# Splitting q after its trip through DRAM, GpSimd's block sums written earlier, and the last norm with squares summed by TensorE

## The chip, the core and the metric

The kernel runs on one core of a Trainium2 chip. The metric is the time of one execution in device microseconds. TensorE (PE in the profile) multiplies, with a separate lane for weight loads (PEld); VectorE (DVE), ScalarE (ACT) and GpSimd (POOL) work on tiles of 128 partitions; SyncE (SP) only issues DMAs here. Each engine runs its own instructions in order and waits for the others through semaphores.

## The reference

One layer of a streaming encoder on 1024 tokens of 1024 channels, float32. `proj` is one wide projection of the normed input; branch A is a gated short convolution, branch B a convolution of width 31 with a layer norm; both are gated, merged and projected, and an FFN and a last norm follow.

```python
h = rms_norm(x, norm_mix_g[l]) * (1.0 + sc1) + sh1
proj = jnp.einsum('bsd,de->bse', h, w_in[l])
b_s, c_s, v_s, v_c, gl_c, gate_br = jnp.split(proj, SPLITS[:-1], axis=-1)

y_a = b_s * causal_dwconv(c_s * v_s, conv_short_w[l])
y_a = jnp.einsum('bsc,cd->bsd', y_a, w_short_out[l])

u = v_c * jax.nn.sigmoid(gl_c)
u = causal_dwconv(u, conv_conf_w[l]) + conv_conf_b[l]
u = jax.nn.silu(layer_norm(u, conf_ln_g[l], conf_ln_b[l]))
y_b = jnp.einsum('bsc,cd->bsd', u, w_conf_out[l])
g_a, g_b = jnp.split(jax.nn.sigmoid(gate_br), 2, axis=-1)
mix = jnp.einsum('bsd,de->bse', g_a * y_a + g_b * y_b, w_o[l])
x = x + g1 * mix

h2 = rms_norm(x, norm_ffn_g[l]) * (1.0 + sc2) + sh2
a, bgate = jnp.split(jnp.einsum('bsd,df->bsf', h2, w_ffn_in[l]), 2, axis=-1)
x = x + g2 * jnp.einsum('bsf,fd->bsd', jax.nn.silu(a) * bgate, w_ffn_out[l])
return rms_norm(x, final_norm_g)
```

`rms_norm(x, g)` is `x * rsqrt(mean(x * x) + EPS) * g`. What the text calls q is `b_s * causal_dwconv(c_s * v_s, conv_short_w)`, the input of `w_short_out`.

## The kernel before

**Three products for one.** Every float32 operand of a matmul is split into a hi part (rounded to the type that TensorE multiplies in one pass, `F32R`) and a lo part (what is left); a block is then hi x hi, lo x hi and hi x lo (`mm3`, lines 281 to 292; the matmuls are those of lines 289, 290 and 292). Weights are split by `split_w` (lines 202 to 212): ScalarE casts a tile of 128 x 1024 to `wh` (line 208), and another engine subtracts it to give `wl` (line 209). `wh` and `wl` have three buffers each, and `next_w` keeps two units ahead of the one in use, so the split of a unit begins when the product three places before it has let go of its buffer.

**The duals.** Most of the input projection is done in twelve duals (lines 722 to 728), each a pair of column blocks multiplied with seven block products in place of eight, in the order `PRODUCTS = "1265734"`. `dual_units` (lines 214 to 238) makes the weights of each product: "1" and "2" are blocks 11 and 12 themselves; "6", "5" and "7" need sums of blocks (`s1` = 21 + 22, 21 + 11, 11 + `s1`, lines 231 to 233), "3" needs 12 + 11 (line 235). All four blocks are loaded when unit "1" is fetched. In the duals of the input projection the lo parts and the sums run on GpSimd (`eng=nc.gpsimd`, line 244), in the FFN's on VectorE. The results leave PSUM through `win_evac` (lines 567 to 631), on ScalarE and VectorE.

**Beside the duals.** VectorE also computes the long convolution (`conv`, lines 648 to 677), whose taps are strung out behind the reads of PSUM, one instruction a tap (line 663); each convolution ends with two ScalarE instructions (line 676), and GpSimd adds it to a running total (`add_conv`, line 683, tile `tot`).

**q.** Four of the pairs are of kind "q". When such a pair's last product is read, the tiles `sc[j]` and `sc[j + 1]` hold q, and `q_store` (lines 541 to 548) splits each half on the spot: ScalarE casts it into a new tile `qs` (line 545), GpSimd subtracts (line 546), and SyncE stores hi and lo together (line 548), 16 stores of 512 KB. In the last dual `q_load` (lines 635 to 638) brings back hi and lo as two loads of 256 KB each, 32 in all, four (j, h) pairs after each of the first four products; the tiles they go to are those that the duals' operands leave. They are the operands of the first product after the duals, `ya` (line 758).

**The end.** The last part of the FFN's output is computed in three pieces of 512, 256 and 256 tokens (`PIECES`), eight steps of 128 channels each (`piece_out`, lines 1069 to 1086): twelve matmuls, an evacuation on VectorE (line 1078), a square on ScalarE (line 1081), and, for what GpSimd will scale, the gain on ScalarE (line 1085). VectorE sums the eight squares (`piece_sum`, line 1090), TensorE sums them over channels with a matrix of ones (`norm_start`, line 410, tile `ss`), ScalarE takes the reciprocal root (line 339), and VectorE refines it in three instructions (`rstd_end`, lines 344 to 346). `piece_scale` (lines 1092 to 1106) multiplies, on GpSimd for the first two pieces and for steps 0, 3 and 5 of the last one (line 1101), else on VectorE (line 1103), and stores in pairs. The norm of a piece is started inside the next piece, after step `NORM_AT` = 2, and finished after step 5; the last piece's comes behind everything.

**What sets the order.** A planner lays out each engine's instructions from the order in which they are written and from when it expects their inputs; `tc.issue_after` puts an instruction behind a given one on the same engine. What is written later can be placed earlier if it is ready earlier.

Of the kernel before, what the change touches and what calls it, by code (L numbers as in the profile page):

```python
# [39 lines left out]
P = 128  # L40
D = 1024
T = 1024
H = 512
# [44 lines left out]

NORM_AT = 2
LAG = 2
POOL_LAST = (0, 3, 5)


# [8 lines left out]
PIECES = [(0, 512), (512, 256), (768, 256)]  # L104


FILL = 272


@with_exitstack  # L110
def block_kernel(ctx: ExitStack, tc: tile.TileContext, x0, xT, c, vecs, ada, w_first, w_plain, w_duals,
# [75 lines left out]
    def raw_tile(n=1024):  # L187

        raws.append(raws.pop(0))
        return raws[-1].tile([P, 1024], F32, tag="raw", name="raw")[:, :n]  # L190
# [23 lines left out]
    def dual_units(mats, n, early=False, eng=nc.vector):  # L214

        a = {}

        def get(*blocks):
            for b in blocks:
                a[b] = load(mats[("11", "12", "21", "22").index(b)], n)  # L220

        def unit(m):
            if early:
                get(*{"1": ("11",), "2": ("12",), "6": ("21", "22", "11"), "3": ("12",), "4": ("22",)}.get(m, ()))
            elif m == "1":
                get("11", "12", "21", "22")
            if m in "12":
                return split_w(a["1" + m], n, (), eng)
            if m == "6":
                a["s1"] = a["22"] if early else raw_tile(n)  # L230
                eng.tensor_tensor(a["s1"], a["21"], a["22"], ALU.add)  # L231
                eng.tensor_tensor(a["21"], a["21"], a["11"], ALU.add)
                eng.tensor_tensor(a["11"], a["11"], a["s1"], ALU.add)
            elif m == "3":
                eng.tensor_tensor(a["12"], a["12"], a["11"], ALU.add)
            return split_w(a[{"6": "11", "5": "s1", "7": "21", "3": "12", "4": "22"}[m]], n, (), eng)

        return {m: (lambda m=m: unit(m)) for m in PRODUCTS}
# [178 lines left out]
    def uc_tile(name, n=T + CK - 1, dt=F32):  # L417
        return ucp.tile([P, T + CK - 1], dt, tag="uc", name=name)[:, :n]
# [120 lines left out]
    q_dram = {}  # L539

    def q_store(j):

        for h in range(2):
            s = uc_tile("qs", T, F32R)
            nc.scalar.copy(s[:, :H], sc[j][:, halves[h]])
            nc.gpsimd.tensor_tensor(s[:, H:], sc[j][:, halves[h]], f32(s[:, :H]), ALU.subtract)
            q_dram[j, h] = dram.tile([P, T], F32, name=f"q{j}{h}")
            nc.sync.dma_start(q_dram[j, h], f32(s))

    def short_conv(j, p):  # L550
        sc[j] = uc_tile(f"sc{j}", T)
# [82 lines left out]

    def q_load(j, h):
        qT[j][h] = t_pair(f"q{j}{h}")
        for t, s in zip(qT[j][h], halves):
            nc.sync.dma_start(f32(t), q_dram[j, h][:, s])


    taps = vec[:, V_CW : V_CW + CK // 2 * 2 * KC].rearrange("p (j two k) -> p j two k", two=2, k=KC)
# [80 lines left out]
    for d in range(n_duals):  # L722
        banks, evac = {}, win_evac(PAIRS[2 * d : 2 * d + 2])
        for i, m in enumerate(PRODUCTS):
            product(banks, m, th[m], evac, y_tile=ps_tile)
            if d == n_duals - 1:
                for n in range(4 * i, min(4 * i + 4, 2 * KC)):
                    q_load(n // 2, n % 2)

    zs = {}  # L730

# [244 lines left out]
    def in_product(d, m):  # L976
        product(in_banks[d], m, ts[m], in_evac(d), y_tile=ps_tile if d == 1 else ps2_tile)
        if d == N_IN - 1:
            group_load(0, m)

    def norm_2_start():
        nonlocal r2
# [86 lines left out]
    def piece_out(i, j):  # L1069
# [12 lines left out]
        if i == LAST and j == KC - 1:  # L1082
            load_rsqrt(act.ins)
        if on_pool(i, j):
            nc.scalar.activation(dst, dst, AF.Copy, scale=col(V_GFIN, j))
        sqs.append(sq)

    def piece_sum(i, j):
# [3 lines left out]
    def piece_scale(i, rf):  # L1092
        at, n = PIECES[i]
        m = H // n
        for j in range(0, KC, m):
            ys = wide_tile("y") if m > 1 else x1[j][:, at : at + n]
            ys = ys.rearrange("p (m n) -> p m n", n=n)
            for d in range(m):
                y, src = ys[:, d], x1[j + d][:, at : at + n]
                if on_pool(i, j + d):  # L1100
                    nc.gpsimd.tensor_tensor(y, src, rf, ALU.mult)
                else:
                    nc.vector.scalar_tensor_tensor(
                        out=y, in0=src, scalar=col(V_GFIN, j + d), in1=rf, op0=ALU.mult, op1=ALU.mult
                    )
            nc.sync.dma_start(outT[j : j + m, :, at : at + n].rearrange("m p n -> p m n"), ys)

    def piece_norm(i, acc):
        return norm_start(acc, "rf", PIECES[i][1], wide_tile)

    for i in range(len(PIECES)):
        acc, sqs = sqs[0] if i else None, []
        lag = LAG if i == LAST else 0
        for j in range(KC):
            piece_out(i, j)
            if j > lag:
                piece_sum(i, j - lag)
            if i and j == NORM_AT:
                norm = piece_norm(i - 1, acc)
            if i and j == NORM_AT + 3:  # L1120
                with tc.issue_after(piece_out.ins):
                    rf = rstd_end(*norm)
                piece_scale(i - 1, rf)
        for j in range(KC - lag, KC):
            piece_sum(i, j)
    piece_scale(LAST, rstd_end(*piece_norm(LAST, sqs[0])))


def _chunks(v):
# [69 lines left out]
```

## Time and profile before

| | |
|---|---|
| median of 3 runs | 1516.14 us (1514.99 to 1517.78) |
| the profiled execution | 1518.37 us, of which the span is 1516.6 us |
| instructions in it | 17958 |
| mean granted TensorE clock | 0.992 |

The span goes from the first to the last instruction of the profiled execution. In rows of a timeline the first number is the start in us from the span's start, the second the duration, and in brackets stands the idle time of the engine before it and what ended it; in groups of the page stand count, busy us and mean ns of one. In rows of windows stand, behind the window and its length, the busy time and count of PE, PEld, DVE, ACT and POOL, then the granted clock, the DMA engines' busy share and GB/s.

The duals of the input projection run from about 128 to 585 us, the product `ya` follows, and the three pieces of the end take the last 50 us.

### The profile page before, as it was taken

The page shows a single profiled execution, that of the slowest core. Times are in us where ns is not written, and L with a number is a line of the kernel's source. Part 1 is how long each engine was busy: PE and PEld are TensorE (multiplying, and loading weights), DVE is VectorE, ACT ScalarE, POOL GpSimd, SP SyncE. Part 2 cuts the span into 40 slices and gives each one's busy share as a digit, 9 for nine tenths or more (in the row PEclk, how much of TensorE's full clock was granted, in tenths as well). Part 3 has the DMA queues.
Part 4 walks back from the last instruction along what each step waited for, and adds up shares of the span by engine and source line. Part 5 has one row for each costly group of instructions (what it writes and reads, how often), then busy time and mean ns, then how long its engine had stood idle before and what let it go on. Part 6 is the DMA issues. An engine that isn't in the chain of part 4 may idle for free.

```text
span 1516.6 us, 17958 instructions
## 1 busy us (share of the span) xinstructions
PE 1480.1 (98%) x6529; PEld 1211.6 (80%) x6529; DVE 1177.6 (78%) x1566; ACT 612.7 (40%) x871; POOL 582.0 (38%) x483
## 2 busy tenths in 40 slices
PE   9999999999998999999999989999999999999996
PEld 5788887877886888888788868888888888888886
DVE  7897898999998881858877798777777665676756
ACT  4654333433332442335335464444444443212234
POOL 0037788788768884320121001000111016535005
PEclk9999999999999999999999999999999999999998
DMA  9512223223222159647765436455554449999303
GB/s 345 207 63 84 84 70 139 70 97 111 98 83 87 66 198 393 242 152 223 251 207 163 143 97 193 156 179 179 181 172 158 155 152 365 354 292 282 124 15 112
DMA packets 87307, 255.66 MB, mean 169 GB/s; under 512 B 10033, under 2 KB 12209, under 8 KB 87218
## 3 DMA queue, kind: packets, MB, share of 16 engines
q1 hardware_dynamic: 46384, 146.30, 28.9%
q0 software_dynamic: 36944, 95.44, 19.1%
q10 hardware_dynamic: 3890, 12.78, 2.1%
q8 instruction: 51, 0.84, 0.2%
q14 instruction: 38, 0.31, 0.1%
HBM read 187.89 MB, written 66.58 MB: 168 GB/s over the span
## 4 chain that ended last, share of the span: by engine, by line
PE 50%; DVE 1%; ACT 1%; issue 0%; DVEq 0%; ACTq 0%
PE x L289 7%; PE x L290 7%; PE x L292 7%; PE z L289 4%; PE z L290 4%; PE z L292 4%; PE y L290 3%; PE y L289 3%; PE y L292 3%; PE mix L289 2%; PE mix L290 2%; PE mix L292 2%; PE yb L289 1%; PE yb L290 1%; PE yb L292 1%
## 5 line engine op out<-in xcount | busy, mean ns | idle before, releaser
L208 ACT CAST wh<-raw 128x1024 fp32r<-128x1024 f32 (+2 forms) x257 | 259.1, 1009 | 422.9 <-PE x L290 107.3
L209 POOL TENSOR_TENSOR wl<-raw,wh 128x1024 fp32r<-128x1024 f32 x92 | 238.0, 2594 | 86.5 <-ACT wh L208 80.1
L209 DVE TENSOR_TENSOR wl<-raw,wh 128x1024 fp32r<-128x1024 f32 (+2 forms) x165 | 188.2, 1141 | 52.4 <-ACT wh L208 50.2
L663 DVE SCALAR_TENSOR_TENSOR c<-diff,vec,c 128x512 f32<-128x512 f32 x248 | 182.3, 749 | 6.4 <-DMA q<-qs 2.6
L942 POOL DMA_DIRECT2D hid<-stage x71 | 37.9, 534 | 356.5 <-DVE stage L329 351.0
L289 PE MATMUL x<-th,wh 128*128 128x512 f32 x336 | 130.8, 389 | 0.0
L292 PE MATMUL x<-th,wl 128*128 128x512 f32 x336 | 130.7, 389 | 0.0
L290 PE MATMUL x<-tl,wh 128*128 128x512 f32 x336 | 130.7, 389 | 0.0
L663 DVE SCALAR_TENSOR_TENSOR c<-u,wsum,c 128x512 f32<-128x512 f32 x112 | 84.0, 750 | 7.1 <-issue 5.1
L292 PE MATMUL x<-t2h,wl 128*128 128x512 f32 x184 | 72.9, 396 | 4.2 <-POOL wl L209 4.2
L289 PE MATMUL x<-t2h,wh 128*128 128x512 f32 x184 | 72.2, 394 | 2.8 <-ACT t2h L328 2.4
L289 PEld LDWEIGHTS x<-th,wh 128*128 128x128 f32 x336 | 63.1, 188 | 13.3 <-issue 0.2
L290 PEld LDWEIGHTS x<-tl,wh 128*128 128x128 f32 x336 | 63.1, 188 | 13.1
L292 PEld LDWEIGHTS x<-th,wl 128*128 128x128 f32 x336 | 63.1, 188 | 13.1
L290 PE MATMUL x<-t2l,wh 128*128 128x512 f32 x184 | 72.5, 394 | 0.0
L231 POOL TENSOR_TENSOR raw<-raw 128x1024 f32<-128x1024 f32 x12 | 29.3, 2439 | 99.5 <-DVE wl L209 95.7
L292 PE MATMUL z<-th,wl 128*128 128x512 f32 x168 | 65.5, 390 | 0.0
L289 PE MATMUL z<-th,wh 128*128 128x512 f32 x168 | 65.4, 389 | 0.0
L290 PE MATMUL z<-tl,wh 128*128 128x512 f32 x168 | 65.4, 389 | 0.0
L328 ACT CAST stage<-g 128x512 fp32r<-128x512 f32 x62 | 38.3, 621 | 56.4 <-DMA hid<-stage 33.4
L270 DVE CUSTOM_DVE_ANT_0 raw<-raw,cs,vec 128x1024 f32<-128x1024 f32 x24 | 34.1, 1424 | 32.3 <-DMA raw<-in_ada 20.0
L329 DVE TENSOR_TENSOR stage<-g,stage 128x512 fp32r<-128x512 f32 x62 | 42.3, 687 | 21.7 <-ACT stage L328 21.6
(799 smaller groups left out, 4095.3 us busy)
## 6 DMA issues: line engine op xcount, KB each, us to landing
hid<-stage POOLq DMA_DIRECT2D x71, 512.0 KB, 4.8
raw<-in_w_fi SPq DMA_DIRECT2D x50, 512.0 KB, 4.2
raw<-in_w_duals SPq DMA_DIRECT2D x48, 512.0 KB, 3.5
th<-hid POOLq DMA_DIRECT2D x71, 256.0 KB, 6.1
tl<-hid POOLq DMA_DIRECT2D x71, 256.0 KB, 6.2
ada<-in_ada SPq DMA_DIRECT2D x24, 512.0 KB, 6.0
raw<-in_ada SPq DMA_DIRECT2D x24, 512.0 KB, 4.7
raw<-in_w_fo SPq DMA_DIRECT2D x24, 384.0 KB, 6.0
```

The lines of the kernel that those rows point to most:

```text
L208: nc.scalar.copy(wh, raw)
L209: lo = lo_engine.tensor_tensor(wl, raw, f32(wh), ALU.subtract)
L231: eng.tensor_tensor(a["s1"], a["21"], a["22"], ALU.add)
L270: nc.vector.tensor_tensor_reduce(out=raw, in0=raw, in1=cs, scale=1.0, scalar=col(V_ADA, b), op0=ALU.mult, op1=ALU.add, accum_out=modc(b),)
L289: nc.tensor.matmul(ps, wh, xh, start=first, stop=False, skip_group_check=again)
L290: nc.tensor.matmul(ps, wh, xl, start=False, stop=False, skip_group_check=again)
L292: mm3.ins = nc.tensor.matmul(ps, wl, xh, start=False, stop=last, skip_group_check=again).ins
L328: nc.scalar.copy(hi, src)
L329: t_split.ins = nc.vector.tensor_tensor(lo, src, f32(hi), ALU.subtract).ins
L663: tap.ins = nc.vector.scalar_tensor_tensor(out=out, in0=src[:, s : s + H], scalar=wt, in1=acc, op0=ALU.mult, op1=ALU.add).ins
L942: nc.gpsimd.dma_start(hid_dram[key], s)
```

## The change

Three edits.

1. `q_store` no longer splits: SyncE stores `sc[j]` whole, 8 stores of 512 KB. `q_load` loads one tile of 256 KB for each (j, h), into the tile that will hold lo; a new `q_split` casts it on ScalarE to hi and subtracts in place on VectorE. The splits are written in the last dual, two products behind their loads.
2. In `dual_units`, when the engine is GpSimd, the sums 21 + 22 and 21 + 11 are written behind the lo part of unit "1", and 11 + `s1` behind that of unit "2"; they stood ahead of the split of unit "6". The FFN's duals keep their order.
3. The end. A piece's norm starts after step 1 of the next one and is finished after step 3. The refinement is rearranged: ScalarE squares the root (times 0.5), VectorE does two instructions with PSUM tiles (`piece_rstd`), and the sign is taken by negated gains `ngf`. For the last piece, VectorE sums only the first five squares; TensorE adds the last three (`APART`) as further matmuls into `ss`. The last factor stays in PSUM, and ScalarE copies it to SBUF for GpSimd (`rp`).

`FILL`, the width of a tile that takes up unused memory, gives back the eight columns that `ngf` needs.

```diff
-NORM_AT = 2
+NORM_AT = 1
 LAG = 2
+APART = 3
-FILL = 272
+FILL = 264
...
+        def sums(which):
+
+            if "1" in which:
+                a["s1"] = a["22"] if early else raw_tile(n)
+                eng.tensor_tensor(a["s1"], a["21"], a["22"], ALU.add)
+            if "3" in which:
+                eng.tensor_tensor(a["21"], a["21"], a["11"], ALU.add)
+            if "2" in which:
+                eng.tensor_tensor(a["11"], a["11"], a["s1"], ALU.add)
...
             if m in "12":
-                return split_w(a["1" + m], n, (), eng)
-            if m == "6":
-                a["s1"] = a["22"] if early else raw_tile(n)
-                eng.tensor_tensor(a["s1"], a["21"], a["22"], ALU.add)
-                eng.tensor_tensor(a["21"], a["21"], a["11"], ALU.add)
-                eng.tensor_tensor(a["11"], a["11"], a["s1"], ALU.add)
-            elif m == "3":
+                w = split_w(a["1" + m], n, (), eng)
+                if eng is nc.gpsimd:
+                    sums("13" if m == "1" else "2")
+                return w
+            if m == "6" and eng is not nc.gpsimd:
+                sums("132")
+            if m == "3":
...
     def q_store(j):
-
-        for h in range(2):
-            s = uc_tile("qs", T, F32R)
-            nc.scalar.copy(s[:, :H], sc[j][:, halves[h]])
-            nc.gpsimd.tensor_tensor(s[:, H:], sc[j][:, halves[h]], f32(s[:, :H]), ALU.subtract)
-            q_dram[j, h] = dram.tile([P, T], F32, name=f"q{j}{h}")
-            nc.sync.dma_start(q_dram[j, h], f32(s))
+        q_dram[j] = dram.tile([P, T], F32, name=f"q{j}")
+        nc.sync.dma_start(q_dram[j], sc[j])
...
     def q_load(j, h):
         qT[j][h] = t_pair(f"q{j}{h}")
-        for t, s in zip(qT[j][h], halves):
-            nc.sync.dma_start(f32(t), q_dram[j, h][:, s])
+        nc.sync.dma_start(f32(qT[j][h][1]), q_dram[j][:, halves[h]])
+
+    def q_split(j, h):
+
+        hi, q = qT[j][h]
+        nc.scalar.copy(hi, f32(q))
+        with tc.issue_after(reads[-1]):
+            nc.vector.tensor_tensor(q, f32(q), f32(hi), ALU.subtract)
...
                     q_load(n // 2, n % 2)
+                for n in range(4 * i - 8, 4 * i - 4):
+                    if 0 <= n < 2 * KC:
+                        q_split(n // 2, n % 2)
...
+    ngf = cp.tile([P, KC], F32, name="ngf")
+    nc.vector.tensor_scalar(ngf, vec[:, V_GFIN : V_GFIN + KC], -1.0, None, ALU.mult)
...
-            nc.scalar.activation(dst, dst, AF.Copy, scale=col(V_GFIN, j))
+            nc.scalar.activation(dst, dst, AF.Copy, scale=ngf[:, j : j + 1])
...
     def piece_scale(i, rf):
         at, n = PIECES[i]
         m = H // n
+        if i == LAST:
+            rp = wide_tile("rp")[:, :n]
+            nc.scalar.copy(rp, rf)
+        else:
+            rp = rf
...
-                    nc.gpsimd.tensor_tensor(y, src, rf, ALU.mult)
+                    nc.gpsimd.tensor_tensor(y, src, rp, ALU.mult)
...
-    def piece_norm(i, acc):
-        return norm_start(acc, "rf", PIECES[i][1], wide_tile)
+    def piece_norm(i, parts):
+
+        n = PIECES[i][1]
+        ss, r, q = (t[:, :n] for t in (ps_tile("ss"), wide_tile("rf"), wide_tile("rq")))
+        for part in parts:
+            nc.tensor.matmul(ss, ones, part, start=part is parts[0], stop=part is parts[-1])
+        rstd_start(ss, eps1, "rf", n, lambda name: r)
+        nc.scalar.activation(q, r, AF.Square, scale=0.5 ** 0.5)
+        return ss, r, q
+
+    def piece_rstd(i, ss, r, q):
+
+        n = PIECES[i][1]
+        t = ps2_tile("rft")[:, :n]
+        nc.vector.scalar_tensor_tensor(out=t, in0=ss, scalar=EPS, in1=q, op0=ALU.add, op1=ALU.mult)
+        out = ps2_tile("rf")[:, :n] if i == LAST else r
+        nc.vector.scalar_tensor_tensor(out=out, in0=t, scalar=1.5, in1=r, op0=ALU.subtract, op1=ALU.mult)
+        return out
...
-            if j > lag:
+            if j > lag and j - lag < KC - APART * (i == LAST):
                 piece_sum(i, j - lag)
             if i and j == NORM_AT:
-                norm = piece_norm(i - 1, acc)
-            if i and j == NORM_AT + 3:
+                norm = piece_norm(i - 1, [acc])
+            if i and j == NORM_AT + 2:
                 with tc.issue_after(piece_out.ins):
-                    rf = rstd_end(*norm)
+                    rf = piece_rstd(i - 1, *norm)
                 piece_scale(i - 1, rf)
-        for j in range(KC - lag, KC):
-            piece_sum(i, j)
-    piece_scale(LAST, rstd_end(*piece_norm(LAST, sqs[0])))
+    piece_scale(LAST, piece_rstd(LAST, *piece_norm(LAST, [sqs[0]] + sqs[KC - APART :])))
```

More of the change, by code (lines that the diff above doesn't have):

```diff
@@ L1100, in piece_scale @@
                 if on_pool(i, j + d):
-                    nc.gpsimd.tensor_tensor(y, src, rf, ALU.mult)
+                    nc.gpsimd.tensor_tensor(y, src, rp, ALU.mult)
                 else:
                     nc.vector.scalar_tensor_tensor(
-                        out=y, in0=src, scalar=col(V_GFIN, j + d), in1=rf, op0=ALU.mult, op1=ALU.mult
+                        out=y, in0=src, scalar=ngf[:, j + d : j + d + 1], in1=rf, op0=ALU.mult, op1=ALU.mult
                     )
             nc.sync.dma_start(outT[j : j + m, :, at : at + n].rearrange("m p n -> p m n"), ys)
-    def piece_norm(i, acc):
-        return norm_start(acc, "rf", PIECES[i][1], wide_tile)
+    def piece_norm(i, parts):
[13 more added lines that the diff above has]
+        return out
     for i in range(len(PIECES)):
```

## Prediction

> **What bounds the kernel now.** First the busy times of the page, then who waits for whom on TensorE alone, then the granted clock in short windows, then GpSimd's and ScalarE's timelines ahead of each wait.
>
> ```profile
> PE 1480.1 (98%) x6529; PEld 1211.6 (80%) x6529; DVE 1177.6 (78%) x1566; ACT 612.7 (40%) x871; POOL 582.0 (38%) x483
> ```
>
> TensorE is the bound: 98% of the span. An engine beside it counts only where TensorE waits for it, or ahead of its first and behind its last product. So the list of its waits is the list of what can be won.
>
> ```profile
> PE x L292 <- POOL wl L209: 7.4, 4, 2.9
> ...
> PE y L292 <- POOL wl L209: 1.1, 1, 1.1
> ```
>
> The columns are total us, times, longest. In all 8.5 us are spent on a lo part of weights that GpSimd had not finished, all in the twelve duals of the input projection. The same view for 340 to 365 us, then for 440 to 490 us:
>
> ```profile
> PE x L292 <- POOL wl L209: 1.4, 1, 1.4
> PE x L292 <- POOL wl L209: 5.7, 2, 2.9
> ```
>
> So there is one wait of 1.4, then 2.9 and 5.7 - 2.9 = 2.8 close together; the remaining 0.3 and 1.1 us come earlier. The two long ones cost more than themselves:
>
> ```profile
> 464.90:468.30 3.40, 2.96 (x7) 2.41 (x8) 2.86 (x5) 1.12 (x3) 3.32 (x3) 0.50 0.00 0
> 482.00:485.40 3.40, 3.40 (x10) 2.66 (x9) 3.40 (x6) 0.59 (x1) 3.30 (x2) 0.51 0.67 216
> ```
>
> The number ahead of the last two is the granted clock: 0.50 and 0.51 for 3.4 us behind each long wait, or 3.4 x 0.5 = 1.7 us of work lost each time. The stage's GpSimd waits are worth 8.5 + 3.4 = 11.9 us.
>
> [...]
>
> What stood ahead of the late lo parts on GpSimd:
>
> ```profile
> 353.37 3.00 POOL L546 TENSOR_TENSOR qs<-sc,qs 128x512 fp32r<-128x512 f32 x2
> 356.33 2.38 POOL L209 TENSOR_TENSOR wl<-raw,wh 128x1024 fp32r<-128x1024 f32 x1
> ...
> 451.95 2.40 POOL L209 TENSOR_TENSOR wl<-raw,wh 128x1024 fp32r<-128x1024 f32 x1 [5.10 <-ACT wh L208]
> 454.31 1.75 POOL L683 TENSOR_TENSOR tot<-tot,u 128x512 f32<-128x512 f32 x1
> 456.02 2.39 POOL L231 TENSOR_TENSOR raw<-raw 128x1024 f32<-128x1024 f32 x1
> 458.38 1.28 POOL L683 TENSOR_TENSOR tot<-tot,u 128x512 f32<-128x512 f32 x1
> 459.64 2.88 POOL L232 TENSOR_TENSOR raw<-raw 128x1024 f32<-128x1024 f32 x1
> 462.48 2.81 POOL L209 TENSOR_TENSOR wl<-raw,wh 128x1024 fp32r<-128x1024 f32 x1
> ...
> 473.80 4.50 POOL L546 TENSOR_TENSOR qs<-sc,qs 128x512 fp32r<-128x512 f32 x2
> ```
>
> The waits of 1.4 and 2.8 us have two subtractions of q right ahead of the lo part: 3.00 and 4.50 us, more than either wait. The wait of 2.9 us is another thing: between two lo parts (451.95 and 462.48) stand two sums of the convolution's total and two block sums, and the first lo part itself began 5.10 us late, for its hi part. ScalarE's timeline says why:
>
> ```profile
> 450.22 0.73 ACT L676 ACTIVATE u<-c,vec 128x512 f32<-128x512 f32 x1 [6.12 <-DVE c L663]
> ```
>
> The end of a convolution, waiting for VectorE, held ScalarE's queue for 6.12 us with the hi cast behind it. q has no part in that.
>
> Note also the order: block sums (L231, L232) run ahead of the lo part at 462.48, though line 231 is written two units later. The planner already moves them to where their inputs are ready.
>
> **The change, part by part.**
>
> (a) q goes through DRAM whole.
>
> ```profile
> L545 ACT CAST qs<-sc x16: 613/620/625, 213.6 to 551.0; 128x512 fp32r<-128x512 f32 x16
> L546 POOL TENSOR_TENSOR qs<-sc,qs x16: 1292/1308/2277, 219.3 to 554.3; 128x512 fp32r<-128x512 f32 x16
> ```
>
> Removed from the duals: 16 x 0.62 = 9.9 us of ScalarE and at least 16 x 1.31 = 21 us of GpSimd, each also an in-order wait on VectorE's sc. The path gains only what ended in TensorE: the waits of 1.4 and 2.8 us and one half-clock stretch, 1.4 + 2.8 + 1.7 = 5.9 us. What is late next is the hi cast behind the ends of the convolutions, which stays. Bounds: 1.4 us (the lo part behind the second pair finds another obstacle) and 11.9 (everything goes).
>
> SyncE issues 8 stores and 16 loads in place of 16 and 32. A store now waits for VectorE's sc itself, and weight loads queue behind it as they did behind GpSimd's subtraction, which came later; I cost this at nothing, its bounds lying inside those above.
>
> Added in the last dual: 16 casts of 0.62 = 9.9 us on ScalarE and 16 subtractions on VectorE, for which the page has a group of the same size; below it the busy times (PE, PEld, DVE, ACT, POOL) of the last dual.
>
> ```profile
> L329 DVE TENSOR_TENSOR stage<-g,stage 128x512 fp32r<-128x512 f32 x62 | 42.3, 687 | 21.7 <-ACT stage L328 21.6
> ```
>
> ```profile
> 547.00:585.00 38.00, 38.00 (x169) 31.45 (x169) 17.76 (x26) 16.25 (x24) 25.44 (x13) 1.00 0.86 311
> ```
>
> At 687 ns that is 16 x 0.687 = 11.0 us of VectorE. The last dual, 547 to 585 us, has VectorE busy 17.76 and ScalarE 16.25 of 38, so both fit (28.8 and 26.2) and cost nothing. Queued behind a cast that waits for its load stand ScalarE's hi casts and sigmoids; but the splits come two products behind their loads, and the loads have half their bytes. DMA, at 0.86 there, gets lighter by 16 x 256 KB of loads; no wait of TensorE in this stretch ends on a DMA, so that wins nothing either.
>
> (b) Block sums written between the lo parts. Same four sums per dual, same engine. As the trace has them between the lo parts already, I take nothing. Bounds: the wait of 2.9 us with its 1.7 and the early 0.3 + 1.1 go as well (6.0 us), or new waits come (below).
>
> (c) The end.
>
> TensorE, ScalarE, VectorE and GpSimd behind the last product, each from its own timeline:
>
> ```profile
> 1501.54 0.28 PE L292 MATMUL y<-th,lwl 128*128 128x256 f32 x1
> 1505.76 1.07 PE L410 MATMUL ss<-sq,ones 128*128 128x256 f32 x2 [3.94 <-DVE sq L1090]
> ```
>
> ```profile
> 1503.54 0.42 ACT L1081 ACTIVATE sq<-x 128x256 f32<-128x256 f32 x1 [0.65 <-DVE x L1078]
> 1503.86 0.19 ACT L352 ACTIVATE rs<-ones 128x1 f32<-128x1 f32 x1
> 1506.87 0.47 ACT L339 ACTIVATE rfr<-ss,eps 128x256 f32<-128x256 f32 x1 [2.82 <-PE ss L410]
> ```
>
> ```profile
> 1503.03 0.48 DVE L1078 SCALAR_TENSOR_TENSOR x<-y,mod,x 128x256 f32<-128x256 f32 x1
> 1503.42 2.28 DVE L1090 TENSOR_TENSOR sq<-sq 128x256 f32<-128x256 f32 x3
> 1507.37 0.56 DVE L344 SCALAR_TENSOR_TENSOR rft<-rfr 128x256 f32<-128x256 f32 x1 [1.67 <-ACT rfr L339]
> 1507.97 0.48 DVE L345 SCALAR_TENSOR_TENSOR rft<-ss,eps,rft 128x256 f32<-128x256 f32 x1
> 1508.49 0.99 DVE L346 SCALAR_TENSOR_TENSOR rfr<-rft,rfr 128x256 f32<-128x256 f32 x1
> 1509.52 3.47 DVE L1103 SCALAR_TENSOR_TENSOR y<-x,vec,rfr 128x256 f32<-128x256 f32 x5
> ```
>
> ```profile
> 1502.94 6.26 POOL L1101 TENSOR_TENSOR y<-x,rfr 128x256 f32<-128x256 f32 x8 [1.70 <-ACT sq L1081]
> 1509.65 2.66 POOL L1101 TENSOR_TENSOR y<-x,rfr 128x256 f32<-128x256 f32 x3 [0.45 <-DVE rfr L346]
> ```
>
> Before: last product over at 1501.54 + 0.28 = 1501.82; evacuated only at 1503.03, as VectorE still had the norm of the piece before; three sums until 1505.70; ss, root, three VectorE steps until 1509.48; five scalings until 1512.99.
>
> After: that norm is taken up two steps earlier, so the evacuation can start at 1501.82 and end at 1502.30; square 0.42, 1502.76 with a gap; TensorE has added the other parts meanwhile and adds the last. From ss to the root took 1506.87 - 1505.76 = 1.11; I take 1.0, 1503.8. Root 0.47 and, on the same engine, the new Square 0.42 with its gap: 1504.75. Two VectorE steps, each like L345's 0.48, as each now has an operand in PSUM: 1505.8. VectorE's five scalings at the old pace end by 1509.3, at 0.48 each at 1508.2. GpSimd's factor first passes ScalarE (0.47, 1506.3), then 2.66: 1509.0. The end of work moves from 1512.99 to about 1509.0: 4.0 us. This needs GpSimd to be through with the piece before, whose eight products now end at 1502.94 + 6.26 = 1509.20; two steps earlier in the loop is enough for the 2.9 us that are needed if the first piece's products, also two steps earlier, don't hold it. Bounds: 2.5 us (GpSimd or TensorE, whose next products queue behind a sum that is now asked for one step earlier, takes 1.5 back) and 4.8 (GpSimd's three products at 6.26/8 each, the last sum at full clock). The one VectorE instruction for the negated gains and the smaller fill tile cost nothing: neither is near a wait of TensorE.
>
> **Sum.** 5.9 + 4.0 = 9.9 us. The profiled execution took 1518.37 (span 1516.6), so 1508.5 by its own time; it lay 2.2 above the median of the runs shown, 1516.14, so the median after is **1506.2**.
>
> **The rivals.**
>
> R1, the rest of the waits goes too: 6.0 more, 1500.2. For it: without q's casts the hi casts come earlier, and any other order at 454 to 462 us that lets the lo part go before one block sum (2.4 to 2.9 us) closes the wait of 2.9. Against: its cause is the convolution's end on ScalarE.
>
> R2, VectorE becomes the bound of the duals: TensorE gets ahead, VectorE's convolution doesn't, and its lag (the 6.12 above) grows by what was won, so that new waits on lo parts eat all but about 1 us there: 1516.14 - 4.0 - 1 = 1511.1, or 1509 to 1513. For it: that row, and VectorE at 78% over all.
>
> R3, the split of q is late.
>
> ```profile
> L620 DVE TENSOR_TENSOR u<-u,sig 128x512 f32<-128x512 f32 x5 | 12.7, 2533 | 0.0
> ```
>
> The same size of operation took 2.53 us here, while GpSimd worked. If 25.44/38 = 0.67 of the subtractions went so, they would take 16 x (0.67 x 2.53 + 0.33 x 0.687) = 30.8 us where 38 - 17.76 = 20.2 are free; the 10.6 us that are over would be TensorE's wait ahead of the short convolution's projection: 1516.8. Against: only the last splits are needed last, and q's j-th block only at the j-th step of that product. [...]
>
> R4, slower: the sums, now ranked ahead of the next lo parts, are run in a lump with the totals. One lump of the kind at 454 to 462 us cost 2.9 + 1.7 = 4.6. It decides from three new ones on (13.8 against 9.9 won); with four, 1506.2 + 18.4 = 1524.6. Against: the planner placed them by readiness before.
>
> **Chances.** Forecast 0.45, R1 0.24, R2 0.20, R3 0.05, R4 0.06. About 0.2% (3 us) is what a measurement of this kernel can tell from no change. Faster by more: forecast, R1, and 0.15 of R2, together 0.84; same: the rest of R2 and R3, 0.10; slower 0.06. The range holds the forecast, R1 and R2: from 1500.2 less 0.8 of the end's upper bound and about 1 us of spread, 1498, to R2's 1513.
>
> **What would show it.** Right: no wait of TensorE on wl near 357 and 480 us, clock 1.00 there; one near 462 still; no qs at all; no wait ahead of ya; ss about 1.2 us behind the last product; the last scaling ending some 7.5 us behind the last product instead of 11.2. Wrong: waits on wl at new places, GpSimd still scaling the second piece when the last factor is ready, a wait on ss one product earlier in each piece.

## The result, and the profile after

The changed kernel takes 1504.92 us, median of six runs (1504.65 to 1507.39), beside 1516.83 us (1514.99 to 1518.97) for the kernel before on the same chip: a ratio of 0.9925, 95% interval 0.9913 to 0.9937, or 11.9 us less by the medians. The forecast was 1506.2, 9.9 us less. The profiled execution took 1504.78, with a span of 1503.0.

A span can be cut where TensorE goes from one stage to the next: the first matmul into `x` (the duals begin), the first into `ya`, the first into `mix`, and the last into `y`. The starts of these four matmuls in the two traces, and the spans' ends, give the lengths of the stages in us:

| | before | after | difference |
|---|---|---|---|
| start to the duals | 114.22 | 114.76 | +0.54 |
| duals | 471.14 | 463.62 | -7.52 |
| `ya` and `yb` | 180.25 | 178.73 | -1.52 |
| `mix` to the last product | 735.93 | 735.63 | -0.30 |
| last product to the end | 15.06 | 10.27 | -4.79 |
| span | 1516.60 | 1503.00 | -13.60 |

(The duals begin at 114 us in the kernel before, not at the 128 named above.) Two stages have moved the way that was forecast, and one that the forecast didn't speak of. First the duals, by TensorE's waits in the kernel after between 300 and 600 us (us in total, times, longest):

```profile
PE x L304 <- POOL wl L211: 3.5, 1, 3.5
PE x L301 <- DVE sig L568: 0.8, 1, 0.8
```

Of five waits on lo parts one is left, and it has grown from 2.9 to 3.5; a wait of 0.8 us on VectorE is new. The granted clock (the third number from the right) in windows around the places of before:

```profile
357.00:361.00 4.00, 4.00 (x19) 3.30 (x19) 3.82 (x7) 0.00 (x0) 0.68 (x1) 1.00 0.48 150
...
462.40:465.80 3.40, 3.40 (x9) 2.63 (x8) 2.52 (x6) 1.72 (x2) 3.40 (x2) 0.50 0.10 42
...
477.00:481.00 4.00, 4.00 (x19) 3.34 (x18) 4.00 (x7) 1.83 (x3) 1.46 (x2) 1.00 0.74 235
```

Near 357 and 480 TensorE is now busy throughout at full clock; the half clock behind the wait that is left has stayed. The matmuls of the duals stand in the same order in both traces, so that the lead of the kernel after can be read off at each product. It changes at six places only: -1.1 us at 242 to 251 us of before, -2.0 at 306 to 312, -1.7 at 357, +0.8 at 458 to 469, -4.7 at 477 to 487, +1.2 at 571 to 585; in all -7.5.

GpSimd's timeline ahead of the wait that is left:

```profile
448.26 2.40 POOL L211 TENSOR_TENSOR wl<-raw,wh 128x1024 fp32r<-128x1024 f32 x1 [7.04 <-ACT wh L210]
450.63 1.75 POOL L696 TENSOR_TENSOR tot<-tot,u 128x512 f32<-128x512 f32 x1
452.33 2.42 POOL L228 TENSOR_TENSOR raw<-raw 128x1024 f32<-128x1024 f32 x1
454.69 1.31 POOL L696 TENSOR_TENSOR tot<-tot,u 128x512 f32<-128x512 f32 x1
455.95 2.87 POOL L230 TENSOR_TENSOR raw<-raw 128x1024 f32<-128x1024 f32 x1
458.77 2.81 POOL L211 TENSOR_TENSOR wl<-raw,wh 128x1024 fp32r<-128x1024 f32 x1
```

It is the row of before again, 3.7 us earlier: a lo part that began 7.04 us late for its hi part, then two totals and two block sums, then the lo part that TensorE waits for. The block sums are written at another place (lines 228 and 230), and run at the same one.

The new wait, from VectorE's timeline in the last dual:

```profile
561.29 2.90 DVE L651 TENSOR_TENSOR q11l<-q11l,q11h 128x512 fp32r<-128x512 f32 x1
...
568.06 2.88 DVE L651 TENSOR_TENSOR q21l<-q21l,q21h 128x512 fp32r<-128x512 f32 x1
570.86 0.68 DVE L651 TENSOR_TENSOR q30l<-q30l,q30h 128x512 fp32r<-128x512 f32 x1
...
572.07 1.28 DVE L568 TENSOR_TENSOR sig<-x,sig 128x512 f32<-128x512 f32 x2
```

The evacuation that TensorE waits for (L568) stands behind four of the new subtractions. One takes 0.68 us by itself and up to 2.90 beside GpSimd. A window with line 651 alone gives all sixteen:

```profile
545.00:590.00 45.00, 17.86 (x16) 1.00 0.95 345
```

17.9 us, where the forecast had 11.0 and its third rival 30.8.

Then the end: TensorE's sum over channels, ScalarE, VectorE and GpSimd behind the last product, which starts at 1492.73, each from its timeline.

```profile
1492.73 0.28 PE L304 MATMUL y<-th,lwl 128*128 128x256 f32 x1
...
1492.86 1.89 PE L1136 MATMUL ss<-sq,ones 128*128 128x256 f32 x8
```

```profile
1494.78 0.47 ACT L351 ACTIVATE rf<-ss,eps 128x256 f32<-128x256 f32 x1 [0.70 <-PE ss L1136]
1495.29 0.42 ACT L1138 ACTIVATE rq<-rf 128x256 f32<-128x256 f32 x1
1496.67 0.37 ACT L1115 COPY rp<-rf 128x256 f32<-128x256 f32 x1 [0.97 <-DVE rf L1147]
```

```profile
1493.05 0.48 DVE L1096 SCALAR_TENSOR_TENSOR x<-y,mod,x 128x256 f32<-128x256 f32 x1 [0.48 <-PE y L304]
1495.73 0.43 DVE L1145 SCALAR_TENSOR_TENSOR rft<-ss,rq 128x256 f32<-128x256 f32 x1 [2.20 <-ACT rq L1138]
1496.20 0.43 DVE L1147 SCALAR_TENSOR_TENSOR rf<-rft,rf 128x256 f32<-128x256 f32 x1
1497.08 2.05 DVE L1126 SCALAR_TENSOR_TENSOR y<-x,ngf,rf 128x256 f32<-128x256 f32 x5 [0.44 <-ACT rp L1115]
```

```profile
1497.12 2.09 POOL L1124 TENSOR_TENSOR y<-x,rp 128x256 f32<-128x256 f32 x3 [1.22 <-ACT rp L1115]
```

VectorE now waits for the last product (0.48 idle) instead of coming 1.2 us late to it; GpSimd is idle for 1.22 us ahead of its last products (0.45 before), so the piece before does not stand in the way. The last scaling ends at 1499.21, 6.2 us behind the last product's end, instead of 11.2.

Last `yb`. VectorE's rows in front of the evacuations of its first half, before and then after:

```profile
714.10 1.28 DVE L270 CUSTOM_DVE_ANT_0 raw<-raw,cs,vec 128x1024 f32<-128x1024 f32 x1 [1.12 <-DMA raw<-in_ada]
```

```profile
705.60 1.28 DVE L282 CUSTOM_DVE_ANT_0 raw<-raw,cs,vec 128x1024 f32<-128x1024 f32 x1
```

Before, VectorE stood 1.12 us for the load of a block of the modulation, with the evacuations queued behind; after, it didn't. TensorE waited 2.1 us there before and 0.5 after. Whether that is the change's doing is a question for the experiments.

### The profile page after: what moved, and what is told of

It is laid out like the page before. It is cut to its first block, busy times and chain, and to the rows that moved or that the text cites. A ratio compares the mean times of both kernels' runs of the same rounds, so it can differ in the third digit from the quotient of the medians.

```text
span 1503.0 us, 17902 instructions
## 1 busy us (share of the span) xinstructions
PE 1477.8 (98%) x6535; PEld 1212.1 (81%) x6535; DVE 1196.9 (80%) x1577; ACT 612.8 (41%) x875; POOL 562.1 (37%) x467
## 4 chain that ended last, share of the span: by engine, by line
PE 50%; DVE 1%; ACT 1%; POOL 0%; issue 0%; POOLq 0%; DVEq 0%; ACTq 0%
PE x L302 7%; PE x L304 7%; PE x L301 7%; PE z L301 4%; PE z L302 4%; PE z L304 4%; PE y L302 3%; PE y L301 3%; PE y L304 3%; PE mix L304 2%; PE mix L302 2%; PE mix L301 2%; PE yb L301 1%; PE yb L304 1%; PE yb L302 1%; POOL y L1124 0%
## 5 line engine op out<-in xcount | busy, mean ns | idle before, releaser
L984 POOL DMA_DIRECT2D th<-hid x71 | 38.0, 535 | 49.6 <-PE x L304 28.6
```

Source lines behind the costliest of these rows:

```text
L984: nc.gpsimd.dma_start(t, hid_dram[key][:, s])
```

## The experiments

The theory: the gain is q's way in the duals and the rearranged end, each by itself, and the block sums' new place does nothing. The first four kernels take the change apart; they ran on one chip beside the kernel before (1516.43 us).

**1. q's way alone**, on the kernel before.

```diff
     def q_store(j):
...
+        q_dram[j] = dram.tile([P, T], F32, name=f"q{j}")
+        nc.sync.dma_start(q_dram[j], sc[j])
...
+                        q_split(n // 2, n % 2)
```

> The kernel before with q's way alone changed (stored whole, split in the last dual). Theory: q's subtractions and casts were what made the lo parts late near 306, 312, 357 and 477 us, so all four waits of TensorE go, the one near 460 us stays (3.5 us and its 1.7 us of half clock), and a new one of about 1 us stands near 571 us, where the splits hold up an evacuation; the product ya begins 7.0 to 7.5 us earlier than before and the time is 1516.8 - 7.5 to 9.0 = 1508 to 1509.5 (the gain of 1.5 us in the product yb is counted in if it belongs to q's way). Rival: it takes the moved sums as well; then one or more of the waits near 306, 312, 357, 477 us are still there and the time is 1511 or more.

Measured: 1509.23, ratio 0.9953 (0.9938 to 0.9968). Its duals took 463.84 us, 7.3 less than before, and its waits between 300 and 600 us are those of the whole change:

```profile
PE x L292 <- POOL wl L209: 3.5, 1, 3.5
PE x L289 <- DVE sig L556: 1.0, 1, 1.0
```

So all of the gain in the duals, the early waits' too, and the new wait belong to q's way.

**2. The block sums alone**, on the kernel before.

```diff
-            if m == "6":
-                a["s1"] = a["22"] if early else raw_tile(n)
...
+                if eng is nc.gpsimd:
+                    sums("13" if m == "1" else "2")
```

> The kernel before with the block sums alone written between the lo parts. Theory: the planner places them as before, so GpSimd's order and the waits of TensorE (8.5 us on lo parts, two stretches of half clock) are those of before: within 1 us of 1516.8. Rival: the sums' place is what cleared the early waits of 0.3 and 1.1 us; then these are gone here and the time is 1 to 2 us shorter.

Measured: 1516.26, ratio 1.000 (0.999 to 1.001). The waits stay:

```profile
PE x L302 <- POOL wl L209: 6.8, 4, 2.7
```

The one of 1.1 us in `y` is there too, and the duals take 470.96 us where they took 471.14.

**3. The end alone**: the kernel after with q's way and the block sums as before.

```diff
-        q_dram[j] = dram.tile([P, T], F32, name=f"q{j}")
-        nc.sync.dma_start(q_dram[j], sc[j])
...
-                if eng is nc.gpsimd:
-                    sums("13" if m == "1" else "2")
```

> The kernel before with the end alone changed. Theory: from the last product of the FFN to the end of the span 10.3 us in place of 15.1, all else as before: 1516.8 - 4.8 = 1512. Rival: part of these 4.8 us hangs on how the pieces before fall in time and doesn't come here: 1513.5 or more.

Measured: 1512.85, ratio 0.9976 (0.9966 to 0.9985); from the last product to the end 10.82 us, 4.2 less than before. That is 0.55 us more than in the whole change, though the scalings stand where they do there: the last store is issued 7.29 us behind the last product's start instead of 6.97, and lands 9.84 instead of 9.30 us behind it. The times are between the theory's 1512 and the rival's 1513.5. By medians q's way is worth 7.2 and the end 3.6 us, 10.8 together of the 11.9: the edits add up within the intervals.

**4. Everything but the block sums.**

```diff
-                if eng is nc.gpsimd:
-                    sums("13" if m == "1" else "2")
...
+            if m == "6":
+                a["s1"] = a["22"] if early else raw_tile(n)
```

> The changed kernel with the block sums written where they were. Theory: the sums do nothing, so this is the changed kernel: 1505, with the same waits. Rival: without the moved sums some of the waits near 306 and 312 us come back: 1506.5 or more.

Measured: 1505.20, ratio 0.9926 (0.9911 to 0.9941), the whole change's. Its duals take 463.43 us, the whole change's 463.62. With experiment 2 this settles the sums: with q's old way and with the new they do nothing that the intervals of 0.1 to 0.15% or the stages could show.

**5. and 6. The wait that is left.** Is it the hi part that comes late, or what GpSimd does between two lo parts? The totals of convolution 5 (L696 in the rows above) are put behind a later lo part, first by one, then by four. The next two and experiments 7 and 8 ran beside the kernel before at 1516.07.

```diff
-        with tc.issue_after(pool_los[(j + 1) * CONV_READS * 7 // (6 * KC) + 5]):
+        with tc.issue_after(pool_los[(j + 1) * CONV_READS * 7 // (6 * KC) + (6 if j == 5 else 5)]):
```

> The changed kernel with the two running totals that stand ahead of the late lo part (at 450.6 and 454.7 us) written one lo part later; nothing else moves. Theory (GpSimd has a backlog there because its first lo part came 7 us late): the wait of 3.5 us near 458 us falls below 1 us, but waits of about 2 and 1 us come up at the next lo parts (near 464 and 472 us), and at most the half clock of 1.7 us is saved: 1503 to 1505. Rival (only what stands ahead of that one lo part matters): wait and half clock go and nothing follows, 1500 to 1501.

Measured: 1503.88, ratio 0.9922 (0.9906 to 0.9939), which can't be told from the whole change. The wait broke up into three:

```profile
PE x L304 <- POOL wl L211: 2.0, 2, 1.1
PE y L304 <- POOL wl L211: 1.9, 1, 1.9
```

The totals now begin at 457.92 us. The lo part that ends there is ahead of them and in time but for 1.1 us; the next one, which begins at 463.25, is behind them and late in its turn (1.9 us), and so is a later one (0.9). The half clock is gone, but the later waits take back most of what that saves: the duals are 463.09 us, 0.5 less than in the whole change. The backlog had only moved on by one, as the theory said.

Experiment 6 has `(9 if j == 5 else 5)` at that place.

> The changed kernel with the same two totals written four lo parts later, behind that of product 5, where GpSimd has time. Theory (backlog): 3.1 us of work leave the stretch in which GpSimd is behind, so no wait over 1 us is left there and the half clock goes: 3.5 + 1.7 - 1 = 4.2 us less than the changed kernel, 1500 to 1501.5. Rival (VectorE's convolution is the bound and the wait only moves): a wait of 2 us or more comes up later in the duals, 1503 or more.

Measured: 1501.00, ratio 0.9908 (0.9893 to 0.9923). GpSimd's timeline at the same place, now without the totals:

```profile
448.09 2.40 POOL L211 TENSOR_TENSOR wl<-raw,wh 128x1024 fp32r<-128x1024 f32 x1 [7.05 <-ACT wh L210]
...
455.76 2.89 POOL L211 TENSOR_TENSOR wl<-raw,wh 128x1024 fp32r<-128x1024 f32 x1
...
472.97 2.54 POOL L696 TENSOR_TENSOR tot<-tot,u 128x512 f32<-128x512 f32 x2
```

The hi part is as late as before (7.05), and the second lo part starts 3.0 us earlier. TensorE's wait is 0.5 us, the clock stays full, the duals take 459.55 us, 4.1 less than in the whole change. With the hi part as late and no totals in front, the wait is half a microsecond; with them it is 3.5. What the totals would cost behind a punctual hi part was not tried.

**7. The split of q one product later.**

```diff
-                for n in range(4 * i - 8, 4 * i - 4):
+                for n in range(4 * i - 12, 4 * i - 8):
```

> The changed kernel with q's splits written three products behind their loads instead of two. Theory: the evacuations that stood behind four subtractions on VectorE now come first, so the wait of 0.8 us near 571 us goes and nothing else: 1504 (0.8 less than the changed kernel, within what a time can tell; the profile decides). Rival: GpSimd's use of the same memory is what makes VectorE late, whatever the order, and the wait stays or moves ahead of ya.

Measured: 1503.69, ratio 0.9923 (0.9908 to 0.9938); the wait near 571 us is gone and the duals are 1.1 us shorter (462.53). The median can't tell that from no change; the stage can, as the five other profiles that have q's new way and the half clock near 462 us lie between 463.43 and 463.85.

**8. The last factor in SBUF**: VectorE writes it there, both engines read it, ScalarE's copy falls away.

```diff
-            rp = wide_tile("rp")[:, :n]
-            nc.scalar.copy(rp, rf)
+            rp = rf
...
-        out = ps2_tile("rf")[:, :n] if i == LAST else r
+        out = r
```

> The changed kernel with the last factor in SBUF: VectorE's second step writes SBUF, GpSimd reads the same tile, ScalarE's copy is gone. Theory (VectorE's two-input instructions are slow while GpSimd works, unless one input is in PSUM): five scalings take 3.5 us instead of 2.05 though they start 0.4 us earlier, so the time from the last product to the end is 11.2 us instead of 10.3. Rival (the copy costs as much as PSUM wins): 10.3 or less.

Measured, in one run of 1505.28 us: 10.49 us from the last product to the end, between the two, and nearer to no loss. The scalings themselves did as the theory said:

```profile
1496.91 3.47 DVE L1125 SCALAR_TENSOR_TENSOR y<-x,ngf,rf 128x256 f32<-128x256 f32 x5
```

```profile
1497.05 2.66 POOL L1123 TENSOR_TENSOR y<-x,rf 128x256 f32<-128x256 f32 x3 [0.90 <-DVE rf L1146]
```

VectorE's five went from 2.05 to 3.47 us and GpSimd's three from 2.09 to 2.66, though they started up to 0.4 us sooner, and the last ends 7.4 us behind the last product's start instead of 6.5. But the span's end hangs on the stores, which SyncE issues one behind the other. The last two issues, in the kernel after and then in this one:

```profile
1499.24 0.92 SPq L1129 DMA_DIRECT2D outT<-y  x2
```

```profile
1499.74 1.05 SPq L1128 DMA_DIRECT2D outT<-y  x2
```

They are through 7.4 us behind the last product's start there and 7.8 here, 0.4 apart. In the kernel after the last two pairs of tiles are ready almost together, so the last store waits for the issue of the one before it, 0.46 us behind; here it is issued right behind the last scaling. The span's end is 0.2 us later here. That is above the spread of the seven profiles whose end is the changed one and that have q's new way (10.25 to 10.27), but less than the 0.55 us by which the last store alone moved the end in experiment 3, so it isn't shown that the copy wins anything in time.

**9. All squares summed by VectorE**, the rest of the end as in the kernel after. This one, 10 and 11 ran beside the kernel before at 1515.39.

```diff
-            if j > lag and j - lag < KC - APART * (i == LAST):
+            if j > lag:
...
+        for j in range(KC - lag, KC):
+            piece_sum(i, j)
+    piece_scale(LAST, piece_rstd(LAST, *piece_norm(LAST, [sqs[0]])))
```

> The changed kernel, with the last piece's squares all summed by VectorE as before, and TensorE given one sum; the rest of the end (early norm, fewer steps behind the root, factor in PSUM) is kept. In the changed kernel ss was ready 1494.08 - 1493.57 = some 1 us behind the last Square's start. Theory (part of the 4.8 us that the end won is the three sums that VectorE no longer makes behind the last product): three sums of 0.42 to 0.56 us in a row on VectorE, of which one can start only behind the last Square, so ss comes 0.6 to 1.7 us later and the time from the start of the last y product to the span's end is 10.9 to 12.0 us instead of 10.27. Rival (the gain is all from the earlier norm, and the sums were only late because VectorE was): 10.3 to 10.6 us.

Measured, in one run of 1505.14 us: 12.14 us from the last product to the end, 1.9 more than the kernel after, a little above the theory's upper end. VectorE's row behind the last evacuation:

```profile
1491.96 2.40 DVE L1108 TENSOR_TENSOR sq<-sq 128x256 f32<-128x256 f32 x3
```

Its last product started at 1491.24. The three sums took 2.40 us, 0.80 each where 0.42 to 0.56 was reckoned, while GpSimd scaled the second piece.

**10. The norm taken up where it was before.**

```diff
-NORM_AT = 1
+NORM_AT = 2
...
-            if i and j == NORM_AT + 2:
+            if i and j == NORM_AT + 3:
```

> The changed kernel with the norm of each piece asked for and finished where it stood before: asked for behind product 2 of the next piece, finished behind product 5, instead of 1 and 3. Theory (taking the norm up earlier is needed, since GpSimd must be through with the second piece): the eight products of the second piece, 6.1 us from 1489.8 on in the changed kernel, start some 2.5 to 3 us later and end near 1498.5, where the last factor is ready at 1497.1; and VectorE has two steps more ahead of the last evacuation. The time from the start of the last y product to the span's end is 11.5 to 13 us instead of 10.27. Rival (nothing waits for it): 10.3 to 10.6 us.

Measured, in one run of 1508.62 us: 11.44 us, 1.2 more than the kernel after, just under the theory's range; its reason holds only in part. VectorE's and GpSimd's rows:

```profile
1496.26 0.47 DVE L1096 SCALAR_TENSOR_TENSOR x<-y,mod,x 128x256 f32<-128x256 f32 x1
...
1500.72 2.04 DVE L1126 SCALAR_TENSOR_TENSOR y<-x,ngf,rf 128x256 f32<-128x256 f32 x5 [0.44 <-ACT rp L1115]
```

```profile
1495.33 5.69 POOL L1124 TENSOR_TENSOR y<-x,rf 128x256 f32<-128x256 f32 x8 [1.25 <-DVE rf L1147]
1500.99 2.08 POOL L1124 TENSOR_TENSOR y<-x,rp 128x256 f32<-128x256 f32 x3
```

The last product started at 1495.41. VectorE evacuates it 0.85 us later, not 0.32, and starts its scalings 5.3 us behind it instead of 4.4, so 1.0 of the 1.2 us is lost on VectorE and what follows it. GpSimd's last products have no idle time ahead of them: they follow the second piece's at once, and that is some 0.2 us more.

**11. The two edits that won, together** (6 and 7), on the kernel after.

> Both of the edits that won by themselves on the changed kernel: convolution 5's two totals stand behind the fifth lo part of the next product instead of the first, and the split of q's blocks comes one product later. Theory (the two waits are independent: one of 3.5 us with a half-clock stretch near 458 us, one of 0.8 us near 571 us): 1501.0 less about 1.0, 1500.0 us (1499.2 to 1500.8), no wait of TensorE on wl above 0.6 us and none on sig. Rival (what the first saves moves the loads and the splits against each other, and the 0.8 us comes back as another wait in the last dual): 1501.0 us or more.

Measured: 1501.39, ratio 0.9901 (0.9882 to 0.9919): no better than experiment 6 that can be told. The duals did gain, 458.61 us, with one wait of 0.9 us on a lo part; but the stage behind them took 181.70, 2.7 more than in experiment 6, with this wait:

```profile
PE yb L301 <- DVE gb L810: 2.1, 2, 1.9
```

So the rival was right that it is lost again, but at another place. That wait need not come from the edit, as it comes and goes between kernels with the same instructions up to there: the kernel after and experiments 8, 9 and 10 differ in the end alone, and have 0.5, 2.1, 0.7 and 2.2 us of it. In experiment 10 VectorE stands 1.57 us, at 707.95, for the load of the block whose modulation ran without idle time in the kernel after. Its load is issued one step ahead, and some executions have it in time.

**12. That modulation one step later**, on top of experiment 11.

```diff
-        if len(loaded) > 1:
+        if len(loaded) > 1 + h:
...
-    modulation_of(*loaded.pop())
+    for one in loaded:
+        modulation_of(*one)
```

> The kernel of the experiment before, with one more edit: in the second half of the projection yb a block of the modulation is multiplied one step later than now, so that VectorE does not stand in front of the first half's eight products with a block whose load has not landed. In the thirteen profiles so far VectorE waited 1.0 to 3.5 us for loads of in_ada between 690 and 735 us, and TensorE's waits on gb there (0.2 to 2.9 us) are that wait less 0.7 to 0.8 each time, though the kernels that differ only at the end have 0.5, 2.1, 0.7 and 2.2. Theory (the load's landing sets TensorE's wait): no wait of TensorE on gb above 0.3 us and no half clock near 712 us; the mean wait of 1.4 us and some of the half-clock stretches of 1.7 us go, and the median is 1499.4 us (1498 to 1500.4), with less spread between its runs than the 2.4 us of the kernel without the edit. Rival (the block holds its buffer one load longer, and a load of weights comes later for it): a wait of TensorE on weights between 690 and 760 us, and 1501 us or more.

Measured: 1497.43 (1495.79 to 1498.48), ratio 0.9876 (0.9860 to 0.9893), beside 1516.62 for the kernel before: faster than both kernels, and below the theory's range. No wait of TensorE on `gb` is left, and `ya` and `yb` take 177.90 us, 3.8 less than in experiment 11. VectorE still waits for loads of `in_ada` between 690 and 735 us, but TensorE no longer waits behind it:

```profile
DVE raw L282 <- DMA raw<-in_ada: 2.2, 3, 1.0
```

Not all of the gain is the edit's, by the profile: the stage from `mix` to the last product, which the edit doesn't touch, is 1.95 us shorter than in experiment 11 (734.23 against 736.18), with one half-clock stretch of 3.4 us near 885 us where experiment 11 has two. (In the thirteen profiles named ahead of this run, TensorE's waits are VectorE's less 0.4 to 0.8 us, not 0.7 to 0.8.)

## Why the prediction was right

**q's way: 5.9 forecast, 7.5 in the trace, 7.2 by itself.** The mechanism was right: the two waits behind pairs of q's subtractions are gone, with one half clock (1.7 + 4.7 us of the ledger above, where 1.4 + 4.5 was forecast). Mis-sized was what else GpSimd's relief would do. The forecast kept the waits of 0.3 and 1.1 us near 306 and 312 and didn't count one of 0.4 near 242, on ScalarE; they went too, worth 3.1 us. That is the first rival, in part. For the 2.0 us near 306 to 312, VectorE's and GpSimd's rows, before:

```profile
274.30 2.89 DVE L620 TENSOR_TENSOR u<-u,sig 128x512 f32<-128x512 f32 x1
```

```profile
273.24 6.20 POOL L209 TENSOR_TENSOR wl<-raw,wh 128x1024 fp32r<-128x1024 f32 x2
...
304.16 2.40 POOL L209 TENSOR_TENSOR wl<-raw,wh 128x1024 fp32r<-128x1024 f32 x1
```

And after:

```profile
274.11 0.68 DVE L627 TENSOR_TENSOR u<-u,sig 128x512 f32<-128x512 f32 x1
```

```profile
301.76 2.41 POOL L211 TENSOR_TENSOR wl<-raw,wh 128x1024 fp32r<-128x1024 f32 x1
```

No subtraction of q stands near the late lo part, those of the pair before having run between 219 and 237 us. It isn't a backlog of GpSimd's own either, as GpSimd stood idle for 5.03 us ahead of 287.13 and for 3.51 ahead of 293.05. What is late is VectorE. Its product `u<-u,sig` took 2.89 us beside two of GpSimd's lo parts; after, GpSimd was through with its lo part at 273.10 and began the next at 274.55, and the product took 0.68. VectorE, busy without a break from there on, ends that convolution 2.4 us later; ScalarE's `u` behind it starts at 292.25 instead of 289.86, and GpSimd's totals and lo parts behind that are late by the same 2.4. In the three profiles with q's old way (before, experiments 2 and 3) the product took 2.88 or 2.89 us, in the eleven with the new way 0.68. So q's way won this by when GpSimd's lo parts fall, which no term of the forecast had. Against it stand 0.8 us at the wait that was left and 1.2 in the last dual; that the sum of the duals came this close, with 3.1 us missed on one side and 2.0 on the other, is in part luck.

**The wait of 2.9 us with ScalarE's late hi part as its cause** stayed, as forecast. But the cause was only half right: the hi part's 7 us of lateness leaves a wait of 0.5 us when the totals are moved away (experiment 6). The first rival's argument, that another order there would close it, was the better one; the change just didn't bring that order.

**The block sums: nothing forecast, nothing found** (experiments 2 and 4). A planner that places by readiness had done it already; no lump, so no fourth rival.

**The split in the last dual at no cost** was wrong by about 1 us: a wait of 0.8, 1.2 in the ledger, of which experiment 7 won back 1.1. The third rival was right that such a subtraction runs slower beside GpSimd, up to 2.9 us for an instruction of 0.68, and wrong about how much that comes to, 17.9 us instead of 30.8. The second rival, VectorE as the bound of the duals, is seen only in small. ScalarE's row at the convolution's end, after:

```profile
446.53 0.73 ACT L689 ACTIVATE u<-c,vec 128x512 f32<-128x512 f32 x1 [7.28 <-DVE c L676]
```

The lag behind VectorE did grow, from 6.12 to 7.28 us, and the wait that is left with it from 2.9 to 3.5, but no other wait came of it.

**The end: 4.0 forecast, 4.8 in the trace, 4.2 in experiment 3.** The sequence came out as written, each step a little sooner. Behind the last product's end the root starts after 1.8 us (2.0 forecast), the factor is ready after 3.6 (4.0), GpSimd has it after 4.0 (4.5). Mis-sized were the scalings: the forecast took 3.47 and 2.66 us from rows of before, with 2.4 for VectorE as the other end; with the factor in PSUM they take 2.05 and 2.09, and experiment 8 brings the old durations back. Experiments 9 and 10 show that the sums on TensorE (1.9 us) and the earlier norm (1.2 us) are both needed, in one profile each. The shorter refinement was not taken out by itself.

**The sum.** The steps were sized 1.6 and 0.8 us too small, which makes 12.3 in place of 9.9; the medians say 11.9. The profiles say 13.6, of which 1.5 are `ya` and `yb`; there the kernel after had its modulation block in time. Kernels that differ in the end alone lie between 178.73 and 180.45 us in this stage, so these 1.5 us can't be put down to the change.

## What to carry to other kernels

An in-order engine that fell behind paid again at its next deadlines (experiment 5: waits of 1.1, 1.9 and 0.9 us in place of one of 3.5). Taking work off an engine also moves what is left there, and that can shorten another engine's instructions far from the work taken off (VectorE's `u<-u,sig`, 2.89 us before and 0.68 after): look at both engines' durations, not only at the waits. Where a late input and queued work both precede a wait, move the queued work first: the lateness alone may cost little (0.5 of 3.5 us in experiment 6). Before a stage's difference between two profiles is put down to the change, see whether kernels with the same instructions in that stage have it too.

## What the runs showed that was not expected

Whether the clock halved behind a wait didn't go by the wait's length alone. In experiment 11 one of 1.9 us on `yb` was followed by 3.4 us at 0.50; in experiment 10 one of 2.0 us at the same place was not, and in experiment 9 one of 3.1 us near 458 was not. In the traces of the kernels before and after there are four and three stretches at half clock ahead of the last product, each 3.41 us long, and within a trace they lie multiples of 3.41 us apart (464.9 and 482.0 us in the kernel before: five of them). Laid on that grid, the stretches around these waits, in the same order (the number behind the comma is TensorE's busy time, the third from the right the clock):

```profile
709.50:712.91 3.41, 1.53 (x7) 0.73 (x5) 3.41 (x5) 0.32 (x1) 0.00 (x0) 1.00 0.74 202
712.91:716.32 3.41, 3.19 (x8) 2.45 (x8) 3.38 (x6) 1.73 (x3) 1.07 (x2) 0.50 0.90 311
```

```profile
715.77:719.19 3.42, 1.57 (x7) 0.95 (x6) 3.42 (x5) 1.23 (x2) 0.30 (x1) 1.00 0.59 178
719.19:722.60 3.41, 3.01 (x12) 2.17 (x13) 3.41 (x7) 1.22 (x2) 1.07 (x2) 1.00 0.93 330
```

```profile
455.70:459.11 3.41, 2.00 (x9) 1.31 (x7) 3.41 (x6) 0.00 (x0) 3.41 (x2) 1.00 0.37 154
459.11:462.52 3.41, 1.70 (x7) 1.42 (x8) 3.34 (x6) 0.00 (x0) 3.33 (x2) 1.00 0.38 154
462.52:465.94 3.42, 3.42 (x16) 2.81 (x15) 2.10 (x6) 2.57 (x3) 3.34 (x3) 1.00 0.00 0
```

The wait of 3.1 us fell across two stretches, which were idle for 1.41 and 1.71 us, and no half clock followed; none followed the one of 2.0 us either, with 1.85 us idle in its stretch; one did follow the wait of 1.9 us, with 1.88. In the traces of before and after, on the same grid, TensorE was idle for 1.9 us or more in each of the seven stretches ahead of one at half clock, and for 1.5 or less in every other at full clock from 100 us to the last product. The idle time within one stretch sorts these cases where the length of the wait doesn't. That it decides is the author's reading: the ends of matmuls are modelled, 1.85 and 1.88 us lie closer than that lets one tell, and no run placed a wait on the grid on purpose. In these traces a wait cost its length, or its length and some 1.7 us (3.41 us at 0.50), and single profiles differ by that.

In the end, ScalarE and VectorE both read the last factor from PSUM, and VectorE's scalings wait 0.44 us for ScalarE's copy to be over, though neither writes it.
